# State space phase tables: the products of each doubling on ScalarE, one scaled copy per group, instead of on VectorE

## The chip, the cores and the metric

One Trainium2 chip; the program runs on one of its cores. The metric is the device time of one execution in microseconds (us). Engines are named as the profile names them: PE is the matrix engine (PEld its weight load), DVE is VectorE, ACT is ScalarE, POOL is GpSimd, SP issues most DMAs.

## What is computed

One decoder layer for a prompt of 1024 tokens and for 8 sample sequences of 8 new tokens each. Four pieces matter here: the input projection, the state space mixer (S5) on 32 groups of 64 complex states, the decode attention of the samples over 8192 cached positions, and what follows (prompt attention, cross-attention, gated MLP). The mixer, cut to its core:

```python
mag = jnp.exp(dt * a_re)
abr = mag * jnp.cos(dt * a_im)
abi = mag * jnp.sin(dt * a_im)
...
# h[l] = a * h[l-1] + b u[l], complex, by an associative scan over 1024 positions
_, _, hr, hi = lax.associative_scan(_cmul_combine, (a_r, a_i, bur, bui), axis=1)
y = (jnp.einsum('blgn,gcn->blgc', hr, p['ssm_c_re'].astype(F32))
     - jnp.einsum('blgn,gcn->blgc', hi, p['ssm_c_im'].astype(F32)))
```

## The kernel before

The program runs in stages: `in` (input projection), `par` (decode attention and, beside it, a chain of side work), `attn`, `mix`, `mem`, `ffn`. Both the decode attention and the state space mixer are generators, and `stage_par` (L1216) takes a piece of each in turn. The side work is, one after the other: the state space groups, the GLU of the mixer, the memory keys and values, the prompt queries, and the weights of the prompt attention.

**State space mixer (`gen_ssm`, L634).** The 1024 positions are 128 chunks of 8. A chunk-to-chunk recurrence with a complex factor is turned into a real scan: the input of each chunk is rotated by a phase, scanned with a real decay, and rotated back. The phases stand in `csn` [128, 2, 4, 128]: cosine and signed sine, for 4 groups of states and 128 chunks. The 32 groups are done in 8 quarters of 4 groups (`NG, NQ = 4, 8`). Per quarter `tables(q)` (L803) builds small weight tables and then `csn`: the first 8 columns are copied from `cs8` (L850, ACT), and four calls `turn(3)` to `turn(6)` (L854) double the filled width from 8 to 128, each by `phases` (L750): the filled columns times the real part and times the imaginary part of one phase factor per state and group (products into `ta` and `tb`), and then a difference and a sum into the next columns. `ta` and `tb` are pieces of `big1` and `big2`, which the table products of the same quarter use too (`t1`, `t2`). `chunks(q)` (L886) reads `csn` in six rotations and in between runs four scans. `csn` has one buffer, so that the copy for the next quarter waits for the last rotation of this one, and `big1` and `big2` have one buffer each. The same `phases` also builds `cs8` once in the stage before, with widths 1, 2 and 4.

**Decode attention (`gen_dec`, L1027).** 16 steps, 4 for each of 4 pairs of samples. A step gathers 4 MB of the paged cache into `kf` (POOL, L1049, two buffers), turns it 32 columns at a time on DVE (`kT`, L1071, nine per step with the one of `rf`, five buffers), multiplies it with the queries on PE (`S`, L1082, one buffer of four PSUM banks), takes the maximum (`mx`, L1103, DVE), four exponentials (`P`, L1110, ACT), turns these (`pt` on PE, L1131, copied to `PT` by ACT, L1132) and multiplies them with the cache rows (`ov`, L1147, PE).

**What sets the order.** Everything from the start to the end of `par` is recorded, and `Order.close` (L239) then plans the order of PE, DVE, ACT and POOL with a table of costs (`Order.cost`, L123): it replays the list a few times, takes the best order found, and pins it. For ACT the cost of an instruction grows with its size alone: 200 + 0.8 n, of which all but 60 holds the engine. The stages behind `par` are ordered by the framework.

The lines of the program that the change touches are L754 and L755; in the profile they count as L643, since `tt` is a helper that stands there. DVE instructions of this step are told by their tiles: `big<-csn,phk` is a product and `csn<-big,big` is a difference or a sum.

Of the kernel before, what the change touches and what calls it, by code (L numbers as in the profile page):

```python
# [13 lines left out]
AF = mybir.ActivationFunctionType  # L14
OP = mybir.AluOpType
# [302 lines left out]
class Kern:  # L318
# [315 lines left out]
    def gen_ssm(self, bank):  # L634

        nc, i, o = self.nc, self.i, self.o
        V, G = nc.vector, nc.gpsimd
# [5 lines left out]
        tt = lambda e, out, a, b, op: e.tensor_tensor(out, a, b, op=op)  # L643
# [76 lines left out]
        for n in (1, 2, 4):  # L720
            bc = lambda a: a[:, None, :].to_broadcast([128, n, 32])
# [28 lines left out]
        def phases(cs, a, pr, pi, ta, tb):  # L750

            n = a.shape[3]
            bc = lambda t: t[:, None, :, None].to_broadcast(list(a.shape))
            tt(V, ta, a, bc(pr), OP.mult)  # L754
            tt(V, tb, a, bc(pi), OP.mult)  # L755
            tt(V, cs[:, 0, :, n:2 * n], ta[:, 0], tb[:, 1], OP.subtract)
            tt(V, cs[:, 1, :, n:2 * n], ta[:, 1], tb[:, 0], OP.add)

# [4 lines left out]
        for k in range(3):  # L763
            n = 1 << k
            phases(cs8, cs8[:, :, :, 0:n], ph[:, 0, k + 1], ph[:, 1, k + 1],
                   *(t.rearrange("p a (g n) -> p a g n", n=4)[:, :, :, 0:n] for t in pt))
# [36 lines left out]
        def tables(q):  # L803
# [50 lines left out]
            def turn(k):  # L854
                n = 1 << k
                phases(csn, csn[:, :, :, 0:n], phk[:, 0, k - 3, gs], phk[:, 1, k - 3, gs], *(t[:, :, :, 0:n] for t in tq))
# [1398 lines left out]
```

## Time and profile before

| | us |
|---|---|
| time, median of 3 runs (1949.39 to 1955.01) | 1950.91 |
| time of the profiled execution | 1952.82 |
| its span | 1951.0 |
| PE busy | 1837.9 (94%) |
| DVE busy | 1105.0 (57%) |
| ACT busy | 806.9 (41%) |
| POOL busy | 522.5 (27%) |

The span is what the trace covers; 1.8 us of the profiled execution lie around it. Busy shares are means over stages that are limited by different things, so the table says little by itself; what counts is the stretch in which the state space quarters run, at about 142 to 385 us. A PE that shows as busy is not a PE at its peak, since the ends of matmuls are modelled and the clock granted to it changes.

### The profile page before, as it was taken

To read this page: it belongs to the slowest core of one execution; us is meant where nothing else is said; L and a number is where in the kernel's file an instruction comes from. 1 tells how busy PE (TensorE), PEld (TensorE's weight loads), DVE (VectorE), ACT (ScalarE), POOL (GpSimd) and SP (SyncE) were. 2 spreads that over 40 slices of the span, in tenths; PEclk is the share of its full clock that TensorE was granted. 3 is DMA by queue.
4 is the path that set the end of the run, shared out by engine and by line. 5 is a ranking of instruction groups with operands and counts; after the bars stand their busy time and mean duration, and the time that the engine had idled before them with its cause. 6 is when DMAs were issued, how large, how long until landed. Compare 5 with 4: busy or idle time off the path is not lost. (4 is left out here: it accounts for less than half of the span.)

```text
span 1951.0 us, 31948 instructions
## 1 busy us (share of the span) xinstructions
PE 1837.9 (94%) x12675; PEld 1442.3 (74%) x12675; DVE 1105.0 (57%) x2013; ACT 806.9 (41%) x1598; POOL 522.5 (27%) x550
## 2 busy tenths in 40 slices
PE   7997988899898999989999989999999999999997
PEld 6884444454654688767778778888888999999775
DVE  3639999775466688843355563434554534434333
ACT  5423333242423488853354443333443433333342
POOL 2332121141211133334211123221244321111554
PEclk9898989899999999999999999999999999999999
DMA  6745354436467511141243453323333522222221
GB/s 200 231 132 198 111 208 150 156 141 261 158 220 259 163 42 28 66 157 33 76 138 133 146 176 101 94 87 97 109 98 97 167 87 87 87 87 80 80 83 59
DMA packets 136597, 248.07 MB, mean 127 GB/s; under 512 B 26912, under 2 KB 91232, under 8 KB 132352
## 3 DMA queue, kind: packets, MB, share of 16 engines
q1 hardware_dynamic: 129120, 170.01, 27.7%
q0 software_dynamic: 7328, 76.03, 10.3%
q8 instruction: 100, 1.64, 0.3%
q14 instruction: 49, 0.40, 0.1%
HBM read 217.26 MB, written 27.42 MB: 125 GB/s over the span
## 5 line engine op out<-in xcount | busy, mean ns | idle before, releaser
L2113 PE MATMUL ps<-xTl,wh 128*128 128x288 f32 (+1 forms) x1056 | 287.8, 327 | 0.0
L2113 PE MATMUL ps<-xTh,wl 128*128 128x288 f32 (+1 forms) x1056 | 287.8, 327 | 0.0
L2113 PE MATMUL ps<-xTh,wh 128*128 128x288 f32 (+1 forms) x1056 | 287.7, 327 | 0.0
L345 POOL TENSOR_TENSOR wl<-st,wh 128x1024 fp32r<-128x1024 f32 (+1 forms) x52 | 116.6, 2243 | 409.0 <-ACT wh L344 409.0
L345 DVE TENSOR_TENSOR wl<-st,wh 128x1024 fp32r<-128x1024 f32 (+1 forms) x52 | 63.5, 1221 | 251.2 <-ACT wh L344 251.2
L344 ACT ACTIVATE wh<-st 128x1024 fp32r<-128x1024 f32 (+1 forms) x104 | 102.6, 993 | 238.6 <-PE ps L2113 217.0
L2113 PEld LDWEIGHTS ps<-xTh,wh 128*128 128x128 f32 x1056 | 179.7, 188 | 13.8
L2113 PEld LDWEIGHTS ps<-xTl,wh 128*128 128x128 f32 x1056 | 179.7, 188 | 13.8
L2113 PEld LDWEIGHTS ps<-xTh,wl 128*128 128x128 f32 x1056 | 179.6, 188 | 13.9
L345 DVE TENSOR_TENSOR wdl<-std,wdh 128x1024 fp32r<-128x1024 f32 x44 | 100.3, 2282 | 147.3 <-ACT wdh L344 147.3
L1082 PE MATMUL S<-kT,Qb 32*64 32x512 f32 x2304 | 155.0, 635 | 14.7 <-DVE kT L1071 8.8
L1071 DVE STREAM_TRANSPOSE kT<-kf 128x1024 f32<-128x1024 f32 x128 | 152.5, 1221 | 28.7 <-DMA kf<-in_cache_kv_dram,idx 19.2
L2064 POOL TENSOR_TENSOR al<-act,ah 128x1024 fp32r<-128x1024 f32 x44 | 106.7, 2426 | 174.0 <-ACT ah L2063 174.0
L354 PE MATMUL ps<-wdh,ah 128*128 128x512 f32 x352 | 139.5, 396 | 0.0
L355 PE MATMUL ps<-wdl,ah 128*128 128x512 f32 x352 | 139.0, 395 | 0.0
L1147 PE MATMUL ov<-kf,PT 128*64 128x256 f32 x1024 | 131.0, 404 | 0.6 <-ACT PT L1132 0.6
L356 PE MATMUL ps<-wdh,al 128*128 128x512 f32 x352 | 126.1, 396 | 0.0
L1147 PEld LDWEIGHTS ov<-kf,PT 128*64 128x64 f32 x1024 | 72.0, 144 | 57.1 <-issue 18.5
L2063 ACT ACTIVATE ah<-act 128x1024 fp32r<-128x1024 f32 (+1 forms) x44 | 49.0, 1113 | 141.5 <-PE ps L355 141.5
L1082 PEld LDWEIGHTS S<-kT,Qb 32*64 32x64 f32 x2304 | 42.5, 135 | 66.7 <-issue 32.4
L1049 POOL DMA_INDIRECT kf<-in_cache_kv_dram,idx x32 | 36.8, 1151 | 174.0 <-PE ov L1147 162.6
L354 PEld LDWEIGHTS ps<-wdh,ah 128*128 128x128 f32 x352 | 66.1, 188 | 17.4 <-issue 0.8
(534 smaller groups left out, 3938.4 us busy)
## 6 DMA issues: line engine op xcount, KB each, us to landing
st<-in_w_gate_dram SPq DMA_DIRECT2D x22, 1024.0 KB
st<-in_w_up_dram SPq DMA_DIRECT2D x22, 1024.0 KB
std<-in_w_down_dram SPq DMA_DIRECT2D x44, 512.0 KB
x<-in_x_prompt_dram SPq DMA_DIRECT2D x16, 512.0 KB
x<-x2d SPq DMA_DIRECT2D x15, 512.0 KB
wst<-in_w_in_dram SPq DMA_DIRECT2D x8, 528.0 KB
xT<-in_xT_dram SPq DMA_DIRECT2D x8, 512.0 KB
ws<-in_w_out_dram SPq DMA_DIRECT2D x8, 512.0 KB
```

Source lines behind the costliest of these rows:

```text
L344: nc.scalar.activation(hi, src, AF.Copy)
L345: (lo_eng or nc.vector).tensor_sub(lo, src, hi.bitcast(F32))
L354: mm(ps, lh, rh, start=start, stop=False)
L355: mm(ps, lh, rl, start=False, stop=False)
L356: mm(ps, ll, rh, start=False, stop=stop)
L1049: G.indirect_dma_start(out=t.rearrange("p k r -> p (k r)"), out_offset=None, in_=rows, in_offset=off)
L1071: V.transpose(t, RF[n] if kb == 8 else KF[n][:, :, :, kb * 32:kb * 32 + 32])
L1082: nc.tensor.matmul(SS[n][half[a], j], Qb[q, kb, 2 * p + a], ts[q, a], start=kb == BLOCKS[0], stop=kb == BLOCKS[-1])
L1147: nc.tensor.matmul(ov[half[a]], PTS[n, g][:, m, half[a]], KF[n][:, a, g * 4 + m], start=g == 0 and m == 0, stop=g == 3 and m == 3)
L2063: nc.scalar.activation(ah[:, :, :nt], a[:, :, :nt], AF.Copy)
L2064: G.tensor_sub(al, a[:, :, :512], ah[:, :, :512].bitcast(F32))
L2113: nc.tensor.matmul(zt[:, :c1 - c0], l[:, k], r[:, k, c0:c1], start=a, stop=b)
```

## The change

```diff
             n = a.shape[3]
             bc = lambda t: t[:, None, :, None].to_broadcast(list(a.shape))
-            tt(V, ta, a, bc(pr), OP.mult)
-            tt(V, tb, a, bc(pi), OP.mult)
+            for t, p in ((ta, pr), (tb, pi)):
+                if n < 8:
+                    tt(V, t, a, bc(p), OP.mult)
+                else:
+
+                    for g in range(a.shape[2]):
+                        nc.scalar.activation(t[:, :, g], a[:, :, g], AF.Copy, scale=p[:, g:g + 1])
             tt(V, cs[:, 0, :, n:2 * n], ta[:, 0], tb[:, 1], OP.subtract)
             tt(V, cs[:, 1, :, n:2 * n], ta[:, 1], tb[:, 0], OP.add)
```

The widths 1, 2 and 4 (the `cs8` table) stay as they are. For the widths 8, 16, 32 and 64 each of the two products becomes four copies on ACT, one per group, each scaled by one number per partition. A copy covers both halves (cosine and sine), so 2 x 8 to 2 x 64 elements. Two DVE instructions become eight ACT instructions per doubling: over 4 doublings and 8 quarters, 64 DVE instructions go and 256 ACT instructions come. The differences and sums stay on DVE. No DMA and no PE instruction is added or removed. Line numbers behind the change grow by 5.

The planner writes a new order. Before the first quarter's doublings nothing moves. Behind it, the quarters stand against the decode steps as before: in both orders the first GLU instruction comes after 80 of the 144 `kT` transposes.

On DVE, in the third quarter, first and second doubling, before the change (`big_2233` and `big_2234` are this quarter's `ta` and `tb`):

```order
L1071 STREAM_TRANSPOSE kT<-kf 128x1024
L643 TENSOR_TENSOR csn<-big_2233,big_2234 128x4x8 x2
L1071 STREAM_TRANSPOSE kT<-kf 128x1024
L643 TENSOR_TENSOR big_2233<-csn,phk 128x8x16
L643 TENSOR_TENSOR big_2234<-csn,phk 128x8x16
L1071 STREAM_TRANSPOSE kT<-kf 128x1024
L643 TENSOR_TENSOR csn<-big_2233,big_2234 128x4x16 x2
L1158 SCALAR_TENSOR_TENSOR O<-O,al,ov 128x256
```

and with the change, the whole of the quarter's doublings (`big_2281` and `big_2282` are `ta` and `tb`):

```order
L643 TENSOR_TENSOR H<-Z,csn 128x4x128
L1076 STREAM_TRANSPOSE kT<-kf 128x1024 x3
L643 TENSOR_TENSOR csn<-big_2281,big_2282 128x4x8 x2
L1076 STREAM_TRANSPOSE kT<-kf 128x1024 x2
L643 TENSOR_TENSOR csn<-big_2281,big_2282 128x4x16 x2
L1076 STREAM_TRANSPOSE kT<-kf 128x1024 x2
L643 TENSOR_TENSOR csn<-big_2281,big_2282 128x4x32 x2
L643 TENSOR_TENSOR hs<-ht,ps 128x32
L643 TENSOR_TENSOR H<-H,A_2294 128x4x128
L643 TENSOR_TENSOR hs<-hs,ht 128x32
L643 TENSOR_TENSOR ta<-bc,f 128x128
```

The products are gone, and transposes that stood between products now stand in pairs between one sum and the next. Behind the last row shown come two more small rows and one transpose, and then the sums of the last doubling.

On ACT, at the softmax of the second decode step and the table copy of the third quarter, before:

```order
L867 ACTIVATE ky<-ps 16x128 x4
L813 ACTIVATE U<-ps 128x512
L1110 ACTIVATE P,ls<-S,nb 128x512 x4
L1120 ACTIVATE al<-nb 128x1
L1132 ACTIVATE PT<-pt 128x512 x2
L850 ACTIVATE csn<-cs_1409 128x8x8
L823 ACTIVATE Cst<-bc,nsgn 128x64
L1132 ACTIVATE PT<-pt 128x512 x2
```

and with the change:

```order
L1115 ACTIVATE P,ls<-S,nb 128x512
L872 ACTIVATE ky<-ps 16x128 x4
L1115 ACTIVATE P,ls<-S,nb 128x512 x3
L1137 ACTIVATE PT<-pt 128x512
L828 ACTIVATE Cst<-bc,nsgn 128x64
L1125 ACTIVATE al<-nb 128x1
L818 ACTIVATE U<-ps 128x512
L855 ACTIVATE csn<-cs_1409 128x8x8
L760 ACTIVATE big_2281<-csn,phk 128x2x8
L760 ACTIVATE big_2282<-csn,phk 128x2x8
```

Four `ky` copies now stand between the first and the second exponential, and the scaled copies follow the table copy. In this quarter the 32 scaled copies are broken by three `PT` copies: one within the first doubling, one just ahead of the third, one within the third.

On ACT, at the first decode step's softmax, before:

```order
L1110 ACT_TABLE_LOAD
L1110 ACTIVATE P,ls<-S,nb 128x512 x4
L1113 ACTIVATE Po,ls<-So,nb 128x64
L1132 ACTIVATE PT<-pt 128x512
L1137 ACTIVATE PTo<-pt 64x128
```

and with the change:

```order
L1115 ACT_TABLE_LOAD
L1115 ACTIVATE P,ls<-S,nb 128x512
L1118 ACTIVATE Po,ls<-So,nb 128x64
L1115 ACTIVATE P,ls<-S,nb 128x512
L1137 ACTIVATE PT<-pt 128x512
L760 ACTIVATE big_1633<-csn,phk 128x2x64
L760 ACTIVATE big_1632<-csn,phk 128x2x64
```

Seven scaled copies of the widest doubling stand between the second and the third exponential of the first step; in the later steps none stands between the exponentials.

## Rows read from the trace of the kernel before

**Rows 1.** The page's second part: busy tenths in 40 slices of 48.8 us.

```profile
PE   7997988899898999989999989999999999999997
...
DVE  3639999775466688843355563434554534434333
ACT  5423333242423488853354443333443433333342
...
PEclk9898989899999999999999999999999999999999
```

**Rows 2.** Busy time of each engine by stretch, with granted clock and DMA.

```profile
core 0: us, PE busy (x) PEld busy (x) DVE busy (x) ACT busy (x) POOL busy (x), PEclk, DMA share, GB/s
142.00:361.00 219.00, 190.32 (x2039) 101.01 (x2023) 214.91 (x431) 70.71 (x196) 41.89 (x37) 0.89 0.46 165
...
390.00:660.00 270.00, 248.60 (x2418) 146.99 (x2416) 166.07 (x261) 100.16 (x223) 54.75 (x51) 0.97 0.56 201
```

**Rows 3.** Groups of instructions by form, DVE, 140 to 390 us: the doublings' products.

```profile
L643 DVE TENSOR_TENSOR big<-csn,phk 128x512 f32<-128x512 f32 x16 | 10.1, 666 | 0.0
...
L643 DVE TENSOR_TENSOR big<-csn,phk 128x256 f32<-128x256 f32 x16 | 6.0, 411 | 0.0
...
L643 DVE TENSOR_TENSOR big<-csn,phk 128x128 f32<-128x128 f32 x16 | 3.7, 267 | 0.0
L643 DVE TENSOR_TENSOR big<-csn,phk 128x64 f32<-128x64 f32 x16 | 2.7, 205 | 0.0
```

**Rows 4.** DVE in order of time, third quarter: start us, us, instruction.

```profile
207.70 0.30 DVE L643 TENSOR_TENSOR big<-csn,phk 128x64 f32<-128x64 f32 x2
207.93 1.23 DVE L1071 STREAM_TRANSPOSE kT<-kf 128x1024 f32<-128x1024 f32 x1
209.09 0.24 DVE L643 TENSOR_TENSOR csn<-big,big 128x32 f32<-128x32 f32 x2
...
210.42 0.44 DVE L643 TENSOR_TENSOR big<-csn,phk 128x128 f32<-128x128 f32 x2
210.79 1.23 DVE L1071 STREAM_TRANSPOSE kT<-kf 128x1024 f32<-128x1024 f32 x1
...
212.78 0.74 DVE L643 TENSOR_TENSOR big<-csn,phk 128x256 f32<-128x256 f32 x2
213.45 0.27 DVE L643 TENSOR_TENSOR ta<-bc,f 128x128 f32<-128x128 f32 x1
...
214.26 1.28 DVE L643 TENSOR_TENSOR big<-csn,phk 128x512 f32<-128x512 f32 x2
215.46 0.67 DVE L643 TENSOR_TENSOR W1T<-BB,pw 128x512 f32<-128x512 f32 x1
```

**Rows 5.** Groups by form, ACT: copies scaled by one number per partition.

```profile
L823 ACT ACTIVATE Cst<-bc,nsgn 128x64 f32<-128x64 f32 x8 | 2.8, 346 | 15.2 <-DVE W L643 14.7 <-DMA bc<-in_ssm_bc_dram 0.4
...
L349 ACT ACTIVATE mxTh<-ps,cols 128x128 fp32r<-128x128 f32 x16 | 5.8, 367 | 10.2 <-DVE mxTl L350 7.7 <-PE ps L1654 2.5
L349 ACT ACTIVATE wqh<-ws,cols 128x512 fp32r<-128x512 f32 x8 | 5.8, 719 | 13.9 <-DMA ws<-in_w_q_dram 13.9
```

**Rows 6.** ACT in order of time: a following instruction, and a scaled pair.

```profile
173.73 0.60 ACT L1132 ACTIVATE PT<-pt 128x512 f32<-128x512 f32 x1 [2.76 <-PE pt L1131]
174.23 0.25 ACT L850 ACTIVATE csn<-cs 128x64 f32<-128x64 f32 x1
...
495.54 0.63 ACT L349 ACTIVATE mxTh<-ps,cols 128x128 fp32r<-128x128 f32 x2 [0.42 <-DVE mxTl L350]
```

**Rows 7.** Who waited for whom, PE, 142 to 361 us: total, times, longest.

```profile
PE pt L1131 <- ACT P L1110: 14.1, 6, 3.9
PE S L1082 <- DVE kT L1071: 6.9, 4, 3.7
PE S L1082 <- ACT P L1110: 2.7, 2, 1.4
```

**Rows 8.** DVE in order of time: the maxima of three decode steps.

```profile
189.09 2.27 DVE L1103 TENSOR_REDUCE mx<-S 128x1 f32<-128x2048 f32 x1
...
219.74 2.27 DVE L1103 TENSOR_REDUCE mx<-S 128x1 f32<-128x2048 f32 x1
...
250.30 2.28 DVE L1103 TENSOR_REDUCE mx<-S 128x1 f32<-128x2048 f32 x1
```

## Prediction

> **What bounds the kernel now.** I read the slices of the page first. The decode attention and its side work lie in slices 3 to 13; there DVE stands at 9 tenths in slices 3 to 6 alone, PE's digit there is no higher than elsewhere, and its granted clock is at 8 or 9 tenths [rows 1]. These four slices are the state space quarters. Next the stretches: from 142 to 361 us DVE is busy 214.9 of 219 us (98%), PE 190.3 (87%) at a granted clock of 0.89, ACT 70.7 (32%), DMA at 0.46 [rows 2]. From 390 to 660 us it is the other way round: PE 92%, DVE 62%. So the quarters are limited by DVE, with PE second, and what follows by PE. The third view is the decode steps: the maxima stand 30.6 us apart [rows 8], and a quarter and a step take about equally long, so both share one full engine. The change takes work off the one that is full and gives it to the one with most room, in the only stretch where DVE limits. The planned order keeps the steps and the quarters against each other as they were, so that a shorter period moves all that follows ahead, by as much as the quarters save.
>
> **What goes.** 64 products leave DVE, 16 of each width: 10.1 + 6.0 + 3.7 + 2.7 = 22.5 us of busy time [rows 3]. Neighbouring DVE instructions overlap a little, so I count what they hold up: in the third quarter the pairs delay the next instruction by 0.23, 0.37, 0.67 and 1.20 us (207.70 to 207.93, 210.42 to 210.79, 212.78 to 213.45, 214.26 to 215.46) [rows 4], 2.47 us per quarter. Eight quarters: 19.8 us, at 9% of the stretch.
>
> **What comes.** 256 copies on ACT, 64 of each of 16, 32, 64 and 128 elements. No row has exactly this form at all sizes. The nearest is `Cst`, also SBUF to SBUF and scaled per partition: 346 ns for 64 elements; `wqh` is 719 ns for 512 [rows 5]. That is 0.83 ns an element, so 306, 319, 346 and 399 ns (estimate from these two). Back to back they may overlap: an instruction behind a `PT` of 0.60 us starts after 0.50, and two `mxTh` of 367 ns take 0.63 together [rows 6], 0.10 us less each time. With the overlap a doubling's eight copies take 1.65, 1.75, 1.97 and 2.39 us, 7.8 us per quarter and 62 us in all; without it 2.45, 2.55, 2.77 and 3.19, 11.0 per quarter and 88 in all. ACT then stands at 133 to 159 of 219 us, 61 to 73%: it doesn't become the full engine. I take the overlap, since the scaled pair shows it.
>
> **The new wait.** In the old program a sum followed its products on the same engine and waited for nothing. Now each doubling goes ACT, DVE, ACT, and DVE waits in order at the sums; queued behind them are the transposes for which PE waits (PE waited 6.9 us for `kT` before [rows 7]). What covers the wait is what the new order puts between two sums, mostly two transposes, 1.16 us each as the next instruction starts (207.93 to 209.09) [rows 4]: 2.3 us. Third quarter: doubling one has three transposes, 3.5 us, against the table copy and eight copies and one `PT`, 0.25 + 1.65 + 0.5 = 2.4 us: covered. Two: 2.3 us against 1.75 and the 0.1 by which the last copy outlasts its slot: covered. Three: 2.3 us against 1.97 + two `PT` of 0.5 + 0.1 = 3.1: DVE stands still for 0.75 us. Four: a transpose and small rows, some 2.4 us, against 2.5: 0.1 us. So 0.85 us per quarter, 6.8 us over eight. The chain through one `csn`, which must be finished, used and freed, grows from about 10 to 16 us per quarter, of 30.6; it isn't what limits.
>
> So DVE gives 19.8 - 6.8 = 13.0 us. The other bound is PE: of 219 us it is idle for 28.7, and 14.1 + 2.7 of that lie between the maximum and the first exponentials of a step [rows 7], where PE has too little else; that remains. 28.7 - 16.8 = 11.9 us can be closed at the clock it had. The two bounds nearly agree; I take 11 us, a little under the smaller.
>
> What it does behind 390 us: the same instructions in nearly the same order on a PE that is 92% busy; the gain is passed on, not multiplied. The framework also turns some rows around in the cross-attention stage, with nothing added; I cost it at nothing, as PE is full there (slices 17 to 23 [rows 1]), with 3 us to either side in the range.
>
> A rule speaks against the change. The row shows that a small ACT copy is nearly all fixed cost: 346 ns for 64 elements, of which 53 are elements [rows 5]. The Trainium skill, VectorE: DVE Perf Modes, section on the TRN2 errata, gives a ScalarE instruction from SBUF a fixed 224 cycles besides its elements and advises tiles of 512 and more; the trace agrees that the cost is per instruction. By its figures alone, and 93 ns for the per-partition scale from ScalarE: Activation LUTs (What ACT_TABLE_LOAD costs), eight copies of the four widths would be 10.5 us per quarter, an estimate by these pages, near my end without overlap. What that would do is the first rival.
>
> **Rivals.** *The bursts outlast their cover.* Without the overlap the four doublings take 2.45, 2.55, 2.77 and 3.19 us of copies; against the same cover DVE stands still for 0, 0.25, 1.5 and 0.8 us, 2.6 per quarter, 20 us in all, and 19.8 - 20 leaves nothing: 1951. For it: nothing in the old trace is a run of eight such copies, and the planner reckons a copy at some 150 to 240 ns of engine time, less than the rows give. Against: the scaled pair [rows 6]. It also stands for the case that the freed slots are lost to waits between PE and DVE.
>
> *DVE alone decides, and PE's clock rises with it.* The clock of 0.89 means that for about 22% of the stretch PE ran at 1.2 instead of 2.4 GHz; that came with a PE that stood still for 13%, whereas at 92% busy it had 0.97 [rows 2]. If fewer holes give the clock back, PE has room, and the whole 19.8 us come: 1931. Against: the holes behind each maximum stay.
>
> *Slower: the exponentials are late.* ACT works in order, and `S` has one buffer, so that a step's last exponential frees the scores of the next. In the new order four `ky` copies, or in the first step seven scaled copies, stand between exponentials: seven of 0.30 us are 2.1 us, and copies of the doublings queue ahead of `PT` as well. If every step's softmax ended 3.2 us later with nothing else for PE to do, that would be 8 x 3.2 = 25.6 us against the 13.0: 12.6 us slower, 1963. It decides from 13.0 / 8 = 1.6 us per step. Against: PE has transposes' products to do meanwhile, and only the first step has scaled copies between its exponentials.
>
> That the change doesn't do what it says I leave out: all four widths of `csn` are 8 or more, and the new order shows them on ACT.
>
> **How the numbers follow.** The sum is made against the profiled execution: span 1951.0 - 11 = 1940.0, time 1952.8 - 11 = 1941.8. The median of the three runs stands 1.9 us under the profiled one, so 1939.9; I predict 1940. A measurement of this kernel tells a change from none from about 0.3%, 5.9 us. Chances: my forecast (6 to 16 us gained) 0.45; the full relief, over 16, 0.13; the bursts outlast their cover, within 5.9 us either way, 0.25; slower by more, 0.17. So faster 0.58, same 0.25, slower 0.17. The range goes from 1930, the full relief with a microsecond over, to 1956, which takes in the case without a gain and the start of the slower one.
>
> **What would show it.** Right: from 142 us on, DVE still over 90% busy but the stretch shorter by about 11 us, the maxima some 29 us apart, 256 scaled copies of about 0.3 us on ACT with some 0.1 us of overlap, and DVE waiting for ACT under 1 us per quarter before the sums. The time behind the quarters should be as long as it was. Wrong: waits of DVE for scaled copies near 20 us in all (first rival), a PE clock well over 0.89 and maxima at 28 us (second), or PE waiting for `P` well over 17 us in the stretch (third). The prediction is wrong altogether if the stretch gets shorter and the end doesn't.

## The result, and the profile after

The changed kernel is slower. Four runs of it took 1975.2 to 1980.8 us, median 1978.9, beside four of the kernel before at 1949.4 to 1959.9, median 1953.0: 26.0 us apart. The ratio on record, on which the rest is built, is smaller, 1.0106 (20.7 us), with a 95% interval of 1.0070 to 1.0142. The profiled execution took 1979.4 us with a span of 1977.6. The 1940 forecast, and its range up to 1956, missed; the forecast of "faster" had the wrong sign.

The page of the kernel after, its second part (40 slices, now of 49.4 us), answers to [rows 1]:

```profile
PE   7897969899898899999989989999999999999997
...
DVE  4639967875455688843345553443554544334433
ACT  5326546442423478852353444333443333333342
...
PEclk9898989899999999999999989999999999999999
```

In slices 3 to 6 (counted from 0) DVE's 9 9 9 9 became 9 9 6 7, ACT's 3 3 3 3 became 6 5 4 6, and PE's digits rose in one of the four and fell in another. The first stretch of [rows 2], busy time by engine (PE, weight loads, DVE, ACT, POOL), granted clock, DMA share and GB/s:

```profile
142.00:361.00 219.00, 179.05 (x1946) 95.84 (x1930) 185.69 (x342) 120.76 (x405) 28.16 (x35) 0.90 0.45 161
```

DVE is 85% busy where it was 98, and PE 82% where it was 87. The time freed on DVE became idle time on DVE, and PE stood still for longer too. The copies themselves, groups by form on ACT from 140 to 390 us, answer to [rows 5]:

```profile
L760 ACT ACTIVATE big<-csn,phk 128x128 f32<-128x128 f32 x64 | 20.9, 392 | 3.3 <-DVE csn L643 2.5 <-DVE hs L643 0.6
L760 ACT ACTIVATE big<-csn,phk 128x64 f32<-128x64 f32 x64 | 16.7, 336 | 2.3 <-DVE csn L643 2.2
L760 ACT ACTIVATE big<-csn,phk 128x32 f32<-128x32 f32 x64 | 15.4, 310 | 3.1 <-DVE csn L643 2.2 <-DVE hs L643 0.7
L760 ACT ACTIVATE big<-csn,phk 128x16 f32<-128x16 f32 x64 | 13.8, 295 | 3.5 <-DVE W1T L643 2.6 <-DVE W L643 0.7
```

295, 310, 336 and 392 ns stand against the 306, 319, 346 and 399 reckoned: the price of a copy was right. What happened is in who waited for whom, from 142 to 420 us (total, times, longest), first DVE's waits, then PE's, which answer to [rows 7]:

```profile
DVE csn L643 <- ACT big L760: 23.9, 20, 3.4
DVE ta L643 <- DMA bc<-in_ssm_bc_dram: 8.0, 1, 8.0
...
PE pt L1136 <- ACT P L1115: 12.3, 6, 5.4
PE pt L1136 <- ACT PT L1137: 10.2, 3, 7.3
```

Three waits are new or larger: 23.9 us at the sums, 8.0 for one load of `bc`, and 10.2 on PE for `PT` (0.8 before). The maxima, which answer to [rows 8]:

```profile
186.48 2.29 DVE L1108 TENSOR_REDUCE mx<-S 128x1 f32<-128x2048 f32 x1
...
215.77 2.29 DVE L1108 TENSOR_REDUCE mx<-S 128x1 f32<-128x2048 f32 x1 [1.18 <-PE S L1087]
...
243.85 2.28 DVE L1108 TENSOR_REDUCE mx<-S 128x1 f32<-128x2048 f32 x1
...
288.90 2.29 DVE L1108 TENSOR_REDUCE mx<-S 128x1 f32<-128x2048 f32 x1
```

The second, third and fourth come 2.6, 4.0 and 6.5 us earlier than before, a little more than the forecast 1.4 us per step. The fifth, 45.0 us behind the fourth, came at 282.8 in the kernel before: now 6.1 us late. One step lost 12.6 us. The attention behind this stage starts 12.9 us late (686.8 against 673.9). Single profiles differ by as much, though: e2 below, with the same program and row up to here as the kernel before, starts it at 687.4, and e1, with those of the changed kernel, at 695.9, 8.5 us later. A second loss lies where nothing was added, between the first transpose of the cross-attention stage and the first matmul of the gated MLP. Those lines, by line (count, ns, first and last start), of the kernel before and then of the one after:

```profile
L1746 PE MATMUL b<-ident,x x72: 222/273/474, 963.0 to 1094.6; 128*128 128x128 f32 x64, 64*128 64x64 f32 x8
L2113 PE MATMUL ps<-xTh,wh x1056: 291/297/487, 1146.6 to 1793.9; 128*128 128x288 f32 x117, 128*128 128x512 f32 x59
```

```profile
L1751 PE MATMUL b<-ident,x x72: 221/272/477, 977.6 to 1111.2; 128*128 128x128 f32 x64, 64*128 64x64 f32 x8
L2118 PE MATMUL ps<-xTh,wh x1056: 291/297/765, 1171.2 to 1820.5; 128*128 128x288 f32 x117, 128*128 128x512 f32 x59
```

1146.6 - 963.0 = 183.6 us before, 1171.2 - 977.6 = 193.6 after: 10.0 us more.

**The fifth step in the trace after.** DVE, SP, POOL and ACT in order of time (start, length; in brackets the idle time before it and who ended it):

```profile
258.35 0.29 DVE L643 TENSOR_TENSOR ta<-bc,f 128x128 f32<-128x128 f32 x1 [8.04 <-DMA bc<-in_ssm_bc_dram]
```

```profile
241.35 4.98 SPq L943 DMA_DIRECT2D y_s<-ky  x8
246.43 0.45 SPq L804 DMA_DIRECT2D bc<-in_ssm_bc_dram  x1
...
244.06 0.95 POOL L1054 DMA_INDIRECT kf<-in_cache_kv_dram,idx  x1 [19.08 <-PE ov L1152]
245.31 0.94 POOL L1054 DMA_INDIRECT kf<-in_cache_kv_dram,idx  x1 [0.30 <-issue]
```

```profile
266.12 0.26 ACT L855 ACTIVATE csn<-cs 128x64 f32<-128x64 f32 x1 [11.91 <-DVE hs L643]
266.41 1.69 ACT L760 ACTIVATE big<-csn,phk 128x16 f32<-128x16 f32 x8
268.52 0.53 ACT L760 ACTIVATE big<-csn,phk 128x32 f32<-128x32 f32 x2 [0.42 <-DVE csn L643]
268.96 0.57 ACT L1137 ACTIVATE PT<-pt 128x512 f32<-128x512 f32 x1
269.44 1.37 ACT L760 ACTIVATE big<-csn,phk 128x32 f32<-128x32 f32 x6
```

SP issues `bc` behind eight `y_s` stores, and right behind two gathers; it is there at 258.3. The new order has `ta` on DVE from 250.3 on, so DVE stands still for 8.04 us, with the scan of the running quarter queued behind it. The rotations behind that scan free `csn`; ACT's next instruction is the copy into `csn`, so ACT idles for 11.9 us, and `PT`, for which PE waits 7.3 us, stands behind that copy and scaled copies. One load passed through three in-order queues.

The load isn't later than it was. It is the seventh of eight; the same load on SP and its `ta` on DVE, in the kernel before, and then in the new row without the copies (e6 below):

```profile
249.54 0.33 SPq L799 DMA_DIRECT2D bc<-in_ssm_bc_dram  x1
...
272.42 0.28 DVE L643 TENSOR_TENSOR ta<-bc,f 128x128 f32<-128x128 f32 x1
```

```profile
241.42 0.39 SPq L803 DMA_DIRECT2D bc<-in_ssm_bc_dram  x1
...
246.77 0.29 DVE L643 TENSOR_TENSOR ta<-bc,f 128x128 f32<-128x128 f32 x1
```

Before, the load went out 3.1 us later than now, and nobody waited, as its `ta` stood 22.9 us behind it. The new row calls for it 22 us earlier. In that row the copies bring the `y_s` stores and the load 5.0 us later (241.4 to 246.4), from just ahead of the gathers (the first at 241.8 in e6) to behind them. So the wait comes from the row and the copies together.

### The profile page after: what moved, and what is told of

Same layout as the page of the kernel before. It is cut to its first block, busy times and chain, and to the rows that moved or that the text cites. A ratio compares the mean times of both kernels' runs of the same rounds, so it can differ in the third digit from the quotient of the medians.

```text
span 1977.6 us, 32158 instructions
## 1 busy us (share of the span) xinstructions
PE 1842.5 (93%) x12675; PEld 1445.5 (73%) x12675; DVE 1086.5 (55%) x1949; ACT 870.4 (44%) x1854; POOL 512.0 (26%) x550
## 5 line engine op out<-in xcount | busy, mean ns | idle before, releaser
L1087 PE MATMUL S<-kT,Qb 32*64 32x512 f32 x2304 | 150.5, 617 | 12.5 <-DVE kT L1076 6.6
L1054 POOL DMA_INDIRECT kf<-in_cache_kv_dram,idx x32 | 32.3, 1010 | 189.0 <-PE ov L1152 176.4
```

Source lines behind the costliest of these rows:

```text
L1087: nc.tensor.matmul(SS[n][half[a], j], Qb[q, kb, 2 * p + a], ts[q, a], start=kb == BLOCKS[0], stop=kb == BLOCKS[-1])
```

## Experiments

In the experiments the kernel before, run beside them, took 1966 to 1970 us (medians of 19 to 31 runs), so each result is its ratio to before, with a 95% interval; 0.001 is 2.0 us. Profiles are single executions and can lie some us off a kernel's median; starts of stages in them are compared with that in mind. "Row" is the order of instructions on PE, DVE, ACT and POOL, and behind the state space stage on SP too; a row is fixed by chaining the instructions in the order of another kernel's program:

```diff
+        xs = [x for x in tr if str(x.engine).split(".")[-1] == e]
...
+        for a, b in zip(order, order[1:]):
+            tc.add_manual_dep(xs[b], xs[a].name, edge, reason="order")
```

**The row behind the stage.** e1 is the changed kernel with the row of before behind the state space stage, e2 the kernel before with the changed kernel's row there.

> The changed kernel as it is up to the end of the state space stage; behind it every engine's instructions stand in the row that they have in the kernel before. Theory A (the row of the cross-attention stage, which the framework's scheduler made anew, costs some 10 us): the stage from its first transpose (L1746) to the first down projection (L2113) is 184 us again instead of 194, and the time is 1979 - 10 = about 1968 us. Rival B (the stage is longer because it begins 13 us later, beside other transfers or another clock; the row is innocent): 1976 to 1980 us, the stage still 194 us. Up to the attention nothing moves under either.

> The kernel before as it is up to the end of the state space stage; behind it every engine's instructions stand in the row of the changed kernel. No product is moved. Theory A (the row alone costs some 10 us): 1951 + 10 = about 1961 us, the cross-attention stage 193 us. Rival B (the row is innocent): 1951 us, the stage 184 us.

Measured: e1 1.0076 (1.0050 to 1.0101), e2 1.0032 (1.0011 to 1.0053). The same two lines, and the stretch from the last start of the one to the first of the other (granted clock last but two), of e1 and then of e2:

```profile
L1751 PE MATMUL b<-ident,x x72: 222/272/473, 987.0 to 1120.8; 128*128 128x128 f32 x64, 64*128 64x64 f32 x8
L2118 PE MATMUL ps<-xTh,wh x1056: 291/297/477, 1173.4 to 1820.6; 128*128 128x288 f32 x117, 128*128 128x512 f32 x59
```

```profile
1120.80:1173.40 52.60, 46.67 (x259) 37.66 (x257) 33.99 (x58) 26.30 (x61) 12.98 (x22) 0.97 0.57 184
```

```profile
L1746 PE MATMUL b<-ident,x x72: 222/272/475, 978.4 to 1111.7; 128*128 128x128 f32 x64, 64*128 64x64 f32 x8
L2113 PE MATMUL ps<-xTh,wh x1056: 291/297/763, 1171.6 to 1821.1; 128*128 128x288 f32 x117, 128*128 128x512 f32 x59
```

```profile
1111.70:1171.60 59.90, 50.10 (x292) 40.08 (x290) 36.71 (x60) 26.83 (x64) 14.26 (x24) 0.90 0.53 169
```

186.4 us with the old row behind the changed stage, 193.2 with the new row behind the unchanged one. The stage's length goes with the row, wherever it begins: theory A, at 7 to 10 us in the profiles and 6.3 by e2's ratio. It took 183.6 to 187.0 us in all fifteen profiles with the old row behind and 193.2 and 193.6 in the two with the new one. The 7 to 8 us lie in its last part: with the new row more matmuls stand there (292 in the line, 259 in the old row), and the granted clock was 0.90 in both profiles, against 0.97 and 1.00 (e1, the kernel before). Which of the moved instructions does it is not shown.

**The late load.** e3 is e1, its row kept inside the stage too, with `bc` loaded ahead:

```diff
-        load(0)
-        load(1)
+        bcs = [new(sp, f"bc{q}", [128, 4, NG, 16]) for q in range(NQ)]
+        for q in range(NQ):
+            nc.sync.dma_start(bcs[q], i["ssm_bc"][:, q])
```

> The changed kernel with the row of before behind the state space stage, the changed kernel's own row inside it, and the eight bc tables loaded to buffers of their own before the first step, so that no bc load stands on SP behind the y_s stores. Theory C (the fifth step lost 12.6 us because DVE waited 8.0 us for a bc load that SP issued late): the wait at ta<-bc is gone, the fifth maximum stands 8 to 12 us earlier, and the time is the one of the kernel with the old row behind (about 1968) less 8 to 12, 1956 to 1960 us. Rival D (ACT's queue, in which scaled copies stand before PT copies, ends last there anyway): the wait moves to the sums or to PE at PT, and the gain is under 4 us, 1964 to 1968 us.

Measured: 1.0020 (1.0003 to 1.0038), 0.0056 or 11 us under e1. DVE in order of time:

```profile
243.24 2.28 DVE L1110 TENSOR_REDUCE mx<-S 128x1 f32<-128x2048 f32 x1
...
250.35 0.29 DVE L643 TENSOR_TENSOR ta<-bc,f 128x128 f32<-128x128 f32 x1
...
280.82 2.29 DVE L1110 TENSOR_REDUCE mx<-S 128x1 f32<-128x2048 f32 x1 [0.35 <-PE S L1089]
```

`ta` no longer waits, and the fifth maximum stands at 280.8 where e1 had 292.0: theory C, 11.2 us. In the profiled executions only 1.1 us of it was left at the attention (694.8 against 695.9); the runs' ratios say that more was kept; e3's profile was of a run slower than its median (1975.4 against 1972.3). The control is the same early loads in the kernel before:

> The kernel before in its own row with the eight bc tables loaded before the first step, and nothing else changed. Control for the early loads: no instruction of before waited more than 0.7 us for a bc load, so nothing should come of it, within 3 us of before. If it is 6 us or more faster, the early loads help by another way (fewer transfers beside the gathers), and what they gave the changed kernel doesn't show that the late bc load was the cause.

0.9981 (0.9955 to 1.0007): no change that can be told from none, though 3.7 us of the 11 could be of this kind.

**Only the copies are added, in the old row.**

> The products are scaled copies on ACT as in the changed kernel, but every other instruction on PE, DVE, ACT and POOL stands in the row of the kernel before, in the state space stage and behind it; the planner chose only where the copies stand between ACT's other instructions. Theory E (the move of the products is worth what was forecast, 19.8 us of DVE time less some 7 us of waits, and the loss comes from the planner's new row): about 1938 to 1945 us, the maxima earlier by 1.6 us per step through all eight quarters. Rival F (copies in ACT's in-order queue make DVE wait at the sums wherever they stand, 24 us and more): 1955 us or more.

Measured 1.0111 (1.0074 to 1.0147), the slowest of the experiments. DVE's waits, 142 to 420 us:

```profile
DVE csn L643 <- ACT big L760: 38.6, 21, 5.0
```

Rival F. The waits at the sums don't come from the planner's new row; without it they are 38.6 us instead of the 23.0 of e1.

**The work left out.** What are the products worth on DVE, and what do the copies cost? e5 takes the products from the kernel before in its row, e6 the copies from the changed kernel in its row:

```diff
+            else:
+                ta = tb = a
```

> The kernel before without the 64 products of the four wide doublings on any engine (the sums read the table's first half in their place, so the phase tables are not the right ones); all other instructions stand on every engine in the row of the kernel before. It measures what the products' time on DVE is worth by itself. Theory A (DVE's time is on the path throughout, as the prediction had it): the attention starts 18 to 20 us earlier than in the kernel before, and the time is 18 to 20 us shorter, a ratio of about 0.990. Rival G (DVE limits only from 142 to 361 us; behind it PE's work ends last, so that part of the gain turns into waits): the maxima of the first eight steps come up to 20 us earlier, but the attention only 6 to 12 us, a ratio of 0.994 to 0.997.

> The changed kernel without its 256 scaled copies (the sums read the table's first half in their place, so the phase tables are not the right ones), every other instruction in the changed kernel's row, and the row of before behind the state space stage. It differs from the changed kernel with the old row behind (1980 us on the chip of the last runs, attention at 695.9) by the copies alone. Theory F (the waits at the sums, 23 us, and the copies ahead of PT and y_s cost the gain): those waits are gone, the attention starts 20 us or more earlier, the time is about 20 us shorter, 0.997 of before. Rival H (the planner's new row itself holds the time, by the late bc load and by the place of the side work): the waits at the sums go, others take their place, and the time is less than 8 us shorter than with the copies.

Measured: e5 0.9987 (0.9963 to 1.0011), e6 0.9905 (0.9874 to 0.9936). The same work is gone from both; in the old row that gave 2.6 us, which the interval doesn't tell from none, in the row that was planned without the products on DVE 18.7. Waits of e5, DVE and PE from 142 to 390 us:

```profile
DVE kT L1074 <- PE S L1085: 18.6, 8, 8.9
...
PE ps L932 <- DMA W<-ky: 10.3, 1, 10.3
```

In the old row DVE arrives early and waits for PE, and PE waits once 10.3 us for the block of `W3` that SP copies from `ky`: SP issued the last of its eight pieces by 328.7, around two gathers, and PE went on at 339.8. The attention starts at 681.2 us against 687.4 in e2, which has the same row with the products: 6.2 us, at rival G's lower end, but within the 13.5 us by which two profiles of one row differed above. The ratio is nearer to 1 than either theory had it. That the transfer ate the gain is likely from this profile, and not shown by a run. In e6 the stretch from 142 to 361 us is

```profile
142.00:361.00 219.00, 197.72 (x2128) 107.29 (x2124) 198.97 (x369) 71.75 (x199) 30.50 (x36) 0.93 0.45 165
```

PE is busy 197.7 of 219 us at a granted clock of 0.93; e2, with before's row in this stretch, has 189.3 at 0.91, and e8 below, newly planned without a relief, 191.7 at 0.91. So with DVE relieved, in a row made for it, PE does have the room.

**The copies' time against the waits for them.** e9 keeps the copies, but the sums don't read them; e12 is e9 with the early loads:

```diff
+            if n >= 8:
+                ta = tb = a
             tt(V, cs[:, 0, :, n:2 * n], ta[:, 0], tb[:, 1], OP.subtract)
```

> The changed kernel in its own row, with the row of before behind the state space stage; the 256 scaled copies run on ACT as before, but the sums read the table's first half in place of the products (so the phase tables are not the right ones), so that DVE waits for no copy. Without copies the same row gave 1951 us (attention at 669.5), with copies and waits 1980 (695.9): 28 us between. Theory F1 (DVE's waits at the sums are what costs): nearly all of the 28 comes back, 1951 to 1958 us, attention at 670 to 677. Theory F2 (the time that the copies take in ACT's in-order queue, ahead of PT, ky and u_all, is what costs, whoever reads them): 1970 us or more. Between them, the two shares are read from the attention's start.

> The changed kernel in its own row (the old row behind the state space stage), the scaled copies run but are not read (the sums read the table's first half, so the phase tables are not the right ones), and the eight bc tables are loaded before the first step. Without the early loads this gave 1.0030 of before, without copies 0.9905. Theory M (what the unread copies cost is mainly the fifth step: ta waits 7.3 us for a bc load that stands on SP behind y_s stores, csn is held meanwhile, and PT copies stand behind csn's copy in ACT's queue, 7.0 us): the fifth maximum comes 8 to 11 us earlier than 284.6, at 274 to 277, and the ratio falls to 0.996 to 0.998. Rival N (the copies' time on ACT costs everywhere): under 4 us gained at the end, 1.001 or more.

Measured: e9 1.0030 (1.0009 to 1.0051), e12 0.9960 (0.9941 to 0.9979). e9 is F2's case: 0.0046 or 9 us comes back when nobody waits for a copy, and 0.0125 stays with the copies. By the ratios that is a quarter of the way from e1 to e6; in the profiles the attention starts at 682.1, 13.8 us before e1's and half of the way, but e9's profile is of its fastest run. More than half of the second part is the late load again: e12 is 0.0070 lower, as theory M had it. Its profile, of its slowest run, doesn't show that gain: the attention starts at 682.1 as in e9, and the fifth maximum moved less than the theory said (280.3 against 284.6, with the fourth 3.1 us later). What is left of e12 over e6, 0.0055, is what 256 copies cost by standing in ACT's queue, with no sum waiting for them; DVE still waited 3.0 us for them where a table product writes into their buffer.

**A better plan for ACT.** The planner reckoned a copy at three quarters of its time:

```diff
+        if e == "Activation" and x.outs[0].bass_ap.tensor.name.startswith("big"):
+            return 190.0 + 0.85 * n, 290.0 + 0.9 * n + 60
```

> The changed kernel planned anew with the scaled copies at their measured price in the planner's table (a copy of 16 elements holds ACT for 204 instead of 153 ns, one of 128 for 299 instead of 242, and its result comes after 364 and 465 instead of 258 and 347), and with the row of before behind the state space stage. Theory J (the planner laid copies and sums too close because it reckoned them at three quarters of their time): the waits at the sums fall from 23 to under 12 us and the time is 8 to 15 us under the 1980 of the same kernel with the old cost, 1965 to 1972, level with before. Rival F2 (256 instructions in ACT's in-order queue cost that much in any row): 1976 us or more, waits at the sums still near 20 us.

Measured 1.0089 (1.0058 to 1.0119): no better. The waits at the sums fell only to 17.7 us. Rival F2. A quarter of the copies, only the widest doubling (`if n < 64` in place of `if n < 8`):

> Only the widest doubling (64 to 128 columns) has its products as scaled copies, 64 of them; the three narrower ones stay on DVE. Planned anew, with the row of before behind the state space stage. DVE's path loses 8 x 1.20 = 9.6 us. Theory F (copies cost by their number, and four doublings a quarter make four round trips between DVE and ACT): with one round trip a quarter the waits at the sums are under 8 us, and the time is 0 to 5 us under that of before. Rival I (any new plan of this stage loses some 10 us, whatever it moves): 5 to 12 us over before.

Measured 1.0035 (1.0010 to 1.0059). The waits at the sums were 3.1 us as theory F said, the time was not: PE waited 9.7 us once for `W<-ky`, as in e5. Does a new plan by itself cost that much?

> The kernel before with one number of the planner changed, the cost of a DVE element (1.05 ns instead of 1.1); no instruction is added, dropped or moved to another engine, but each engine's row up to the end of the state space stage is planned anew. The row behind it is the one of before. Theory: the time depends on the work and less on which of many near plans is taken: within 4 us of before. Rival I (the plan of before is a lucky one, and a new plan of the same work costs as much as the whole change did): 8 us or more over before.

Measured 0.9991 (0.9972 to 1.0010): 1.8 us less than before, so rival I falls for this plan. That plans of one program can differ by more, e11 and e15 show below.

**Another engine.** The products on POOL, whole, two instructions per doubling:

```diff
+            e = V if n < 8 else G
+            tt(e, ta, a, bc(pr), OP.mult)
+            tt(e, tb, a, bc(pi), OP.mult)
```

> The products of the four wide doublings as two whole instructions each on POOL, 64 in all, planned anew, the row of before behind the state space stage. POOL was busy 12 of 98 us there. Without products at all the changed kernel's row gave 0.9905 of before. Theory K (what spoiled the move was ACT's queue, and POOL has room): DVE keeps the relief, and the time is 5 to 15 us under before, ratio 0.992 to 0.997. Rival L (POOL is slower per element, DVE waits at the sums, and the gathers that POOL issues come late behind the products): 0 to 20 us over before.

Measured 0.9951 (0.9932 to 0.9969): 9.6 us faster than before, the best of all kernels that compute the tables. A group on POOL by form, 142 to 400 us, and the stretch from 142 to 361:

```profile
L643 POOL TENSOR_TENSOR big<-csn,phk 128x512 f32<-128x512 f32 x16 | 18.3, 1162 | 10.0 <-DVE hs L643 6.6 <-DVE csn L643 3.3
```

```profile
142.00:361.00 219.00, 191.41 (x2067) 105.69 (x2067) 202.96 (x365) 71.19 (x198) 71.95 (x101) 0.93 0.46 165
```

The widest product takes 1162 ns on POOL, 666 on DVE [rows 3] and the pair of them took eight copies of 392 ns on ACT; but POOL does little else here than issue gathers, and DVE waits 5.6 us at the sums. The Trainium skill, Perfetto Trace Analysis (Optimizing Scalar/DVE Operations), warns that moving work between DVE and GpSimd might not help, since they share a read port of SBUF. It helped here, though the trace agrees that the two hold each other up (POOL, then DVE, in order of time, and the same DVE instruction with no product beside it):

```profile
207.13 1.46 POOL L643 TENSOR_TENSOR big<-csn,phk 128x512 f32<-128x512 f32 x1 [1.47 <-DVE hs L643]
```

```profile
207.60 1.03 DVE L643 TENSOR_TENSOR hs<-hs,ht 128x32 f32<-128x32 f32 x1
```

```profile
182.95 0.18 DVE L643 TENSOR_TENSOR hs<-hs,ht 128x32 f32<-128x32 f32 x1
```

DVE's instruction ends with POOL's, at 208.6. From 142 to 400 us the eight of this form took 391 ns on average, where the kernel before has 177, and the eight of `ht<-h,p` 416, where it has 208; added up over DVE's two-input instructions (TENSOR_TENSOR) beside products it is 5.7 us. Transposes took 1221 ns, 1224 before. The sums themselves wait for the products of their table, and so don't run beside them.

POOL in the row of the changed kernel, and POOL with early loads:

> The products as 64 whole instructions on POOL, but every other instruction of PE, DVE, ACT and POOL in the row of the changed kernel, and the old row behind the state space stage; the planner chose only where the products stand on POOL. In the same row the copies on ACT gave 1.0076 of before and no products 0.9905. Theory K (ACT's queue is what spoiled the move): 0.993 to 0.999, the waits at the sums under 10 us, no wait of DVE for bc. Rival O (a row made for ACT's copies holds the time wherever the products are; POOL's gathers come late): 1.004 or more.

> The products on POOL, planned anew as in the version that gave 0.9951 of before, and the eight bc tables loaded before the first step. No wait for bc is in that version's trace, so by the theory that loads matter only where someone waits for them it is 0.993 to 0.997 again; the planner sees other loads and makes another row, which may move it by 0.002. If early loads help by themselves, 0.991 or less.

Measured: e13 1.0010 (0.9989 to 1.0031), e15 0.9997 (0.9968 to 1.0025). e13 lies between its theories: in one and the same row POOL is better than ACT by 0.0066, with 8.7 us of waits at the sums, but a row made for ACT doesn't give POOL's best. e15 did not repeat e11: its planner made another row, 0.0046 worse, more than the 0.002 allowed for that. So the 9.6 us are those of one plan: that POOL is better here than ACT is shown, by e13 against e1, and that it beats DVE by as much in any plan is not.

## Why the prediction was wrong

Put in order, the runs are a ladder, each one cause taken away from the one before it:

| | ratio to before | us of that step |
|---|---|---|
| changed kernel | 1.0106 | |
| old row behind the stage (e1) | 1.0076 | 5.9 |
| `bc` loaded ahead (e3) | 1.0020 | 11.0 |
| sums don't wait for copies (e12) | 0.9960 | 11.8 |
| no copies on ACT (e6) | 0.9905 | 10.8 |

The steps are differences of ratios times 1968 us, each with 5 to 9 us of uncertainty. The first ratio is from other runs than the rest, so that its step is not clear of noise by itself; e2 has the same cost at 6.3 us, clear of it. Up to 3.7 us of the second could be early loads helping in another way (e14). e6 needs no early load, since nobody waits for one there.

- **What goes: right in size.** 19.8 us of relief was reckoned from 22.5 of busy time; e6 gained 18.7. But that the gain is passed on because the planned order keeps steps and quarters against each other was no general reason: with the old row kept (e5) only 2.6 us came. Of these two rows only the one planned for the change gave the relief.
- **PE as the second bound, 11.9 us: wrong.** e6 gained 18.7, with PE at 197.7 us busy in the stretch and a clock of 0.93 (e2: 189.3 and 0.91). That is the second rival's case, which had 0.13; the copies took it away.
- **What comes: right.** Eight copies of 16 elements took 1.69 us (1.65 reckoned), and the overlap was there.
- **The new wait: the step that failed first.** 0.85 us per quarter was reckoned from the third, 6.8 in all; the trace has 1.1, 1.1, 1.2, 1.4, 5.7, 2.0, 9.3 and 2.2 us, 23.9 in all, of which e12 puts some 12 on the path. The first four quarters were close. The cover was wrong: "mostly two transposes" between two sums holds in the third quarter, and 15.0 of the 23.9 us lie in the fifth and the seventh, where at five of the eight doublings no transpose stands on DVE between the sums before and these. The seventh quarter, DVE in order of time:

```profile
332.35 0.36 DVE L643 TENSOR_TENSOR csn<-big,big 128x64 f32<-128x64 f32 x2 [1.84 <-ACT big L760]
336.14 0.49 DVE L643 TENSOR_TENSOR csn<-big,big 128x128 f32<-128x128 f32 x2 [3.43 <-ACT big L760]
336.55 0.75 DVE L643 TENSOR_TENSOR W<-Cst,pw 128x576 f32<-128x576 f32 x1
340.30 0.76 DVE L643 TENSOR_TENSOR csn<-big,big 128x256 f32<-128x256 f32 x2 [3.00 <-ACT big L760]
```

  Besides, other copies (`ky`, `PT`, `u_all`) stand between the scaled ones, there as in other quarters. One quarter was taken for all eight.
- **ACT's time: costed at nothing, 10.8 us.** ACT at 61 to 73% "doesn't become the full engine" was right (it stood at 55%) and beside the point: 10.8 us stay with copies that no sum waits for, by what queues behind them.
- **SP's queue: not looked at, 11.0 us.** The new row calls for a `bc` load 22 us earlier than the old one, and the copies bring `ky`, so `y_s`, and so that load 5.0 us later than the same row has them without copies. The prediction followed DVE's and ACT's queues and not SP's, whose order the planner doesn't plan either.
- **The cross-attention row: costed at nothing, with 3 us to either side; 5.9 to 10 us.** A row that changes where no work does is still a change; "PE is full there" was no reason against a loss (PE was busy for 169.0 of the 183.6 us before).
- **The slower rival** (0.17) had the right sign, not the mechanism: PE's waits for `P` were 12.3 us, where 17 and more were to show it. Nor was it the first rival's: the waits came near its 20 us, but not by copies without overlap.
- The rule that was weighed, the Trainium skill's advice in VectorE: DVE Perf Modes (TRN2 errata) against small ScalarE tiles, came out at 10.5 us of copies per quarter; eight in a row of the four widths took 1.69, 1.80, 2.02 and 2.45 us, 8.0 in all, since they overlap, which that sum left out. The small copies were a bad choice in this case, but by the queue and not by that sum.

## What to carry to other kernels

To move work from a full engine to an idle one, read what stands in the receiving engine's queue and who waits behind it, in every repetition and not in one; busy shares don't show it. Follow the delay through the queues that only issue transfers, and look at every stretch whose order the change moves, the ones without added work too. A few whole instructions on a slower but quiet engine can beat many cheap ones on an engine that others wait for (here by 13 us in the same row, e13 against e1). Price a change in the row that the planner makes for it, and expect a new plan alone to move the time: two plans of the products on POOL, one with the early loads, lie 9 us apart.

## What the hardware showed that was not expected

- A small transfer issued behind gathers came late: the `bc` load, issued at 246.4 right behind two gathers, was there at 258.3, 11.9 us later, while the DMA engines moved 371 to 379 GB/s. In e6 the same load, issued 0.4 us ahead of the gathers, was there within 5.4 us. The last piece of `W3` in e5, issued by 328.7, was there at 339.8, 11 us later.
- Scaled copies overlap in a run of their kind, and with a `PT` copy behind them (in the changed kernel five from 205.28 take 1.30 us, and `PT` starts at 206.49), but not beside the `ky` copies of L940. Eight of 64 elements in a row took 2.02 us, 0.25 each; alternating with those `ky` copies one held ACT for 0.38, no less than its own length. ACT in order of time:

```profile
335.09 0.35 ACT L760 ACTIVATE big<-csn,phk 128x64 f32<-128x64 f32 x1
335.47 0.27 ACT L940 ACTIVATE ky<-ps 8x128 f32<-8x128 f32 x1
```

- A two-input instruction of DVE that started while POOL multiplied was held to the end of the product: 1.03 us in place of 0.18 in e11, above (from 207.60 to 208.63, where the product runs from 207.13 to 208.59). Transposes were not held (1221 ns on average, 1224 before).
